# Second feed-forward product also as seven block products, two pairs of tiles at a time, with sums of the middle channels parked in DRAM

## The chip, the cores and the metric

One core of one Trainium2 chip runs the whole kernel. Times are device microseconds. A run's time is that of one execution; the kernel before is given by the median of three runs. One further execution was recorded by the hardware profiler, and all rows below come from it. PE is TensorE, DVE VectorE, ACT ScalarE, POOL GpSimd, SP SyncE; the DMAs are issued from SP's queue, those that add into their target from POOL's.

## The reference, cut to what matters

One layer of a hybrid decoder on 512 tokens with 1024 channels, float32. The mixers ahead are untouched by the change; it concerns the feed-forward part:

```
x = x + merged
gate, up = split(rms_norm(x, norm2_g) @ w_ffn_in, 2)    # (512,1024) @ (1024, 2*2816)
x = x + (silu(gate) * up) @ w_ffn_out                   # (512,2816) @ (2816,1024)
```

The weights come as float32 from DRAM. Every product is formed from three float32r products (high half of the weights by high half of the activations, high by low, low by high), so each 128x128 weight tile is split on the chip: ACT casts it to its high half, DVE subtracts that from the tile to get the low half, and PE multiplies.

## The kernel before, in words

All activations lie channels by tokens, so a matmul has a 128x128 weight tile as its stationary side and up to 512 tokens as its moving side. Up to the residual the kernel runs the mixers and w_out with `Dense.__call__` (L1292): 4 weight tiles are loaded with one DMA of 256 KB, split, and multiplied with all 512 tokens.

**The first product** uses `SevenProducts` (L1310): the two halves of the input channels, the two column blocks of a pair (one tile of gate columns, one of up columns) and the two halves of the tokens make a 2x2 by 2x2 block product, which needs seven block products and not eight. A block product here is a *piece*: 4 weight tiles, three matmuls each, of 256 tokens: 12 matmuls. The pieces come in the order p1, p5, p6, p3, p7, p2, p4 (`seven`, L1395). Their weights are: p1 block g0; p5 the sum s of two blocks, formed by a plain load and a DMA that adds the second block; p6 is s plus g0 (added in place by DVE, L1415); p3 is that plus g1; p7 is g0 plus another block, which a DMA adds into g0's buffer once p6 has read it (`third`, L1455); p2 is g1 and p4 is u1. The seven results are added up in the readers r1 to r4, and r4 multiplies silu(gate) by up and splits the result into the activations of the second product, kept in 11 arenas.

Two pairs run interleaved, piece by piece, 11 such couples for 22 pairs. The raw blocks lie in a ring of 12 buffers of 512 columns (L1359), the split ones in rings of 6; `run` (L1491) makes (adds, casts, subtracts) five pieces ahead of PE.

**The second product** (L1301 to L1303 with act) is plain: 8 output tiles by 22 input tiles by three matmuls of 512 tokens, 48 weight blocks with one DMA, one cast and one subtraction each. `take_out` (L1746) scales, adds the residual, which lies in DRAM, and writes.

Every engine runs its own list of instructions in order; a wait in front of one holds all behind it. The lists are made by a scheduler at build time, so they differ from the order in which the code issues.

Of the kernel before, what the change touches and what calls it, by code (L numbers as in the profile page):

```python
# [23 lines left out]
P = 128  # L24
# [67 lines left out]
class Env:  # L92


    def __init__(self, ctx, tc):
# [26 lines left out]
        self.pools["s"] = Slots("slot", self.early + cut(arenas[NARENA - 3:]))  # L122
# [61 lines left out]
    def leave_mixers(self):  # L184

        assert not self.scopes
        self.mctx.close()
        self.spool = self.later.enter_context(self.tc.tile_pool(name="fpool", bufs=1, reuse_waits="tile"))
        self.phase = "f"
        free = [b for n in ("pd", "prw", "ps") for b in self.pools[n].free]  # L190
        assert len(free) == 8
        for n, k in (("pd", 4), ("ps", 4)):
            self.pools[n] = Slots(n, [free.pop(0) for _ in range(k)])

# [1014 lines left out]
class Dense:  # L1209
# [23 lines left out]
    def ring(self, tag, dt, n):  # L1233

        tiles, at = self.rings.setdefault(tag, ([], [0]))
        if len(tiles) < n:
            at[0] = len(tiles)
            tiles.append((self.E.spool if self.E.phase else self.E.cpool).tile([P, KB * P], dt, name=self.E.uid(tag)))
        t = tiles[at[0] % len(tiles)]
        at[0] += 1  # L1240
        return t

# [67 lines left out]
class SevenProducts:  # L1310
# [10 lines left out]
    H, N, AHEAD = 4, 256, 5  # L1321

    def __init__(self, E, dense, act_hi, act_lo):
# [5 lines left out]
        self.raws, self.turn = None, 0  # L1329
# [26 lines left out]
    def block(self, w, k):  # L1356
        return self.dense.blocks(w, KD, P)[k]

    def raw(self):  # L1359

        E = self.E
        if self.raws is None:
# [7 lines left out]
    def load(self, w, k, t=None, add=False):  # L1370
        E, nc = self.E, self.E.nc
        t = self.raw() if t is None else t
        v = t.rearrange("p (k n) -> p k n", n=P)
        if add:
            nc.gpsimd.dma_start(v, self.block(w, k), accum_op=ALU.add)
        else:
            nc.sync.dma_start(v, self.block(w, k))
        return t

    def split(self, w):  # L1380
        d = self.dense
        hi, lo = d.ring("wh", F32R, WB[1] + 1), d.ring("wl", F32R, WB[1] + 1)
        self.E.split(w, hi, lo)
        return hi, lo

    def matmuls(self, ps, w, b, js, first, last):
        nc = self.E.nc
        for j in js:
            c = slice(j * P, (j + 1) * P)
            for n, (x, y) in enumerate(((0, 0), (0, 1), (1, 0))):  # L1390
                nc.tensor.matmul(ps, w[x][:, c], b(y, j), start=first and j == js[0] and n == 0,  # L1391
                                 stop=last and j == js[-1] and n == 2, skip_group_check=True)


    def seven(self, o, i, wg, wu):  # L1395
# [4 lines left out]
        act = lambda k, t: (lambda y, j: self.act[y][:, H * k + j, t])  # L1400
        tee = lambda i: (lambda y, j: self.t[y][:, i, j])

        def piece(name, make, bank, x, first, read):
            def mm():
                if bank not in o:
                    o[bank] = E._take("pf", (P, 512), True)
                self.matmuls(o[bank][:, 0:N], o[name], x, range(H), first, True)

            def mk():
                o[name] = self.split(make())  # L1410
            return mk, mm, read

        def sum_(other, after=None):
            def f():
                V.tensor_tensor(o["s"], o["s"], o[other], ALU.add)  # L1415
                if after:
                    after()
                return o["s"]
            return f

        def r1():
            o["k"], o["n"] = (E.slot("sp_k", keep=True) for _ in range(2))
            nc.scalar.copy(o["k"][:, a], o["x"][:, 0:N])  # L1423

        def r5():
            nc.scalar.copy(o["n"][:, b], o["y"][:, 0:N])

        def r6():
            nc.scalar.copy(o["k"][:, b], o["x"][:, 0:N])

        def r3():
            V.tensor_tensor(o["k"][:, b], o["k"][:, b], o["y"][:, 0:N], ALU.add)
            E.free(o["y"])

        def r7():
            nc.scalar.copy(o["n"][:, a], o["x"][:, 0:N])
            V.tensor_tensor(o["k"][:, b], o["k"][:, b], o["n"][:, b], ALU.add)
            V.tensor_tensor(o["n"][:, b], o["n"][:, a], o["n"][:, b], ALU.add)

        def r2():  # L1440
            V.tensor_tensor(o["k"][:, a], o["k"][:, a], o["v"][:, 0:N], ALU.add)
            E.free(o["v"])
            V.tensor_tensor(o["k"], o["k"], self.R, ALU.mult)
            nc.scalar.activation(o["k"], o["k"], AF.Silu)

        def r4():
            t, n = o["k"], o["n"]
            V.tensor_tensor(t[:, a], t[:, a], o["x"][:, 0:N], ALU.mult)
            E.free(o["x"])
            V.tensor_tensor(t[:, b], t[:, b], n[:, b], ALU.mult)  # L1450
            E.free(n)
            E.split(t, self.out[0][i], self.out[1][i], -1.0)
            E.free(t)

        def third():  # L1455
            self.load(wu, 0, o["g0"], add=True)

        return [piece("p1", lambda: o["g0"], "x", act(0, a), True, r1),
                piece("p5", lambda: o["s"], "y", act(0, b), True, r5),
                piece("p6", sum_("g0", third), "x", tee(0), False, r6),  # L1460
                piece("p3", sum_("g1"), "y", act(1, b), True, r3),
                piece("p7", lambda: o["g0"], "x", tee(1), False, r7),
                piece("p2", lambda: o["g1"], "v", act(1, a), True, r2),
                piece("p4", lambda: o["u1"], "x", tee(2), False, r4)]

    def first(self, f):
        for i in range(f, min(f + 2, len(self.pairs))):
            o, (wg, wu) = self.os[i], self.pairs[i]
            o["g0"], o["s"] = self.load(wg, 0), self.load(wu, 0)
            self.load(wu, 1, o["s"], add=True)  # L1470

    def rest(self, f):
        for i in range(f, f + 2):
            o, (wg, wu) = self.os[i], self.pairs[i]
            o["g1"], o["u1"] = self.load(wg, 1), self.load(wu, 1)

    def begin(self, pairs, n):


        self.pairs, self.os = pairs, [{} for _ in pairs]  # L1480
        self.pieces, self.at, self.made = [], {}, n
        for f in range(0, len(pairs), 2):
            self.at[len(self.pieces)] = f
            for both in zip(*[self.seven(self.os[i], i, *pairs[i]) for i in (f, f + 1)]):
                self.pieces += both
# [363 lines left out]
```

## Time and profile before

| | us |
|---|---|
| runs (median of 3; lowest to highest) | 1004.62 (1004.23 to 1010.87) |
| the profiled execution | 1011.66 |
| its span, first to last instruction | 1009.9 |
| its mean granted TensorE clock | 0.988 |

The profiled execution's own time is 1.74 us more than its span and 7.04 us above the median. Shares of busy time on the page are means over stages with different limits; the stages that matter here are the end of w_out (until 663.6 us in the span), the first product (to 885.7 us) and the second (to 1005.5 us).

### The profile page before, as it was taken

Reading aid. Unit: us, or ns where it says so; the run is one execution under the profiler, and the core shown is the slowest. Engines: PE = TensorE matmul, PEld = TensorE weight load, DVE = VectorE, ACT = ScalarE, POOL = GpSimd, SP = SyncE. Lnnn points to the kernel's source line nnn. Section 1 sums busy time; section 2 is a strip of 40 time slices with the busy share of each in tenths; the row PEclk is TensorE's granted clock in tenths of the full one; section 3 lists DMA queues with packets and bytes.
Section 4 is the critical chain, followed back from the end, with each engine's and each line's share of the span. In section 5 each row is a group of like instructions: output and inputs, shape, how many; then the busy total and the mean of one; then the engine's idle time right before and its main releaser. Section 6 shows DMA issues by size and latency. Waiting matters only on the chain.

```text
span 1009.9 us, 17883 instructions
## 1 busy us (share of the span) xinstructions
PE 970.1 (96%) x6416; PEld 824.2 (82%) x6416; DVE 754.3 (75%) x1941; ACT 473.5 (47%) x978; POOL 143.3 (14%) x176
## 2 busy tenths in 40 slices
PE   7989999899999999999999999989999999999998
PEld 5777777676779777888887788879999999988886
DVE  6899676789994789977867655679989998943331
ACT  6534333434342566446446324566666666632220
POOL 2021120422420001000000332011211221000000
PEclk9999899999998999999999999999999999999999
DMA  7325242221431334252448864476776677354440
GB/s 241 116 53 133 64 110 78 84 56 53 100 96 40 95 105 116 84 156 75 154 149 270 273 194 159 138 178 165 151 163 175 152 153 170 79 155 123 131 136 27
DMA packets 105593, 129.95 MB, mean 129 GB/s; under 512 B 45376, under 2 KB 47296, under 8 KB 105504
## 3 DMA queue, kind: packets, MB, share of 16 engines
q1 hardware_dynamic: 99168, 117.28, 38.7%
q0 software_dynamic: 6336, 11.54, 7.4%
q8 instruction: 50, 0.82, 0.3%
q14 instruction: 39, 0.32, 0.1%
HBM read 109.90 MB, written 18.88 MB: 128 GB/s over the span
## 4 chain that ended last, share of the span: by engine, by line
PE 77%; DVE 15%; DMA 3%; ACT 2%; issue 2%; POOL 1%; SPq 0%; DVEq 0%; ACTq 0%; POOLq 0%
PE bank L1391 21%; PE bank L1302 13%; PE bank L1303 13%; PE bank L1301 13%; DVE wl L1230 2%; DMA ar<-in_w_ffn_in 1%; DMA ar<-ymix 1%; PE bank L468 1%; PE bank L479 1%; PE bank L1188 1%; PE bank L262 1%; PE bank L630 1%; PE bank L1285 1%; PE bank L1286 1%; PE bank L1287 1%
## 5 line engine op out<-in xcount | busy, mean ns | idle before, releaser
L1229 ACT CAST wh<-wr 128x512 fp32r<-128x512 f32 x198 | 120.4, 611 | 208.8 <-PE bank L1302 163.6
L1230 DVE TENSOR_TENSOR wl<-wr,wh 128x512 fp32r<-128x512 f32 x198 | 136.8, 693 | 82.8 <-ACT wh L1229 82.3
L1301 PE MATMUL bank<-act_hi,wh 128*128 128x512 f32 x360 | 150.5, 418 | 7.8 <-ACT wh L1229 5.9
L1302 PE MATMUL bank<-act_lo,wh 128*128 128x512 f32 x360 | 149.7, 416 | 0.8 <-DVE act_lo L257 0.7
L1303 PE MATMUL bank<-act_hi,wl 128*128 128x512 f32 x360 | 149.6, 416 | 0.0
L1391 PE MATMUL bank<-sp_t,wh 128*128 128x256 f32 x528 | 97.5, 285 | 1.1 <-ACT ar L1423 0.8
L1391 PE MATMUL bank<-act_hi,wh 128*128 128x256 f32 x352 | 98.0, 278 | 0.0
L1391 PE MATMUL bank<-act_hi,wl 128*128 128x256 f32 x352 | 97.7, 278 | 0.1
L1391 PE MATMUL bank<-act_lo,wh 128*128 128x256 f32 x352 | 97.5, 277 | 0.0
L1301 PEld LDWEIGHTS bank<-act_hi,wh 128*128 128x128 f32 x360 | 70.0, 195 | 22.7 <-ACT wh L1229 5.9
L1391 PEld LDWEIGHTS bank<-sp_t,wh 128*128 128x128 f32 x528 | 82.7, 193 | 1.5 <-ACT ar L1423 1.0
L1302 PEld LDWEIGHTS bank<-act_lo,wh 128*128 128x128 f32 x360 | 70.0, 194 | 16.4 <-DVE act_lo L257 3.5
L1303 PEld LDWEIGHTS bank<-act_hi,wl 128*128 128x128 f32 x360 | 70.0, 194 | 14.4 <-issue 0.6
L1391 PE MATMUL bank<-sp_t,wl 128*128 128x256 f32 x264 | 75.2, 285 | 0.0
L1301 PE MATMUL bank<-act,wh 128*128 128x512 f32 x176 | 68.5, 389 | 0.0
L1302 PE MATMUL bank<-act,wh 128*128 128x512 f32 x176 | 68.5, 389 | 0.0
L1303 PE MATMUL bank<-act,wl 128*128 128x512 f32 x176 | 68.5, 389 | 0.0
L1391 PEld LDWEIGHTS bank<-act_hi,wl 128*128 128x128 f32 x352 | 66.2, 188 | 0.7 <-DVE wl L254 0.7
L1391 PEld LDWEIGHTS bank<-act_hi,wh 128*128 128x128 f32 x352 | 66.4, 189 | 0.3
L1391 PEld LDWEIGHTS bank<-act_lo,wh 128*128 128x128 f32 x352 | 66.4, 189 | 0.0
L253 ACT CAST wh<-ar 128x512 fp32r<-128x512 f32 x79 | 48.2, 622 | 28.1 <-DMA ar<-in_w_ffn_in 18.1
L254 DVE TENSOR_TENSOR wl<-ar,wh 128x512 fp32r<-128x512 f32 x79 | 53.1, 685 | 9.4 <-ACT wh L253 8.9
(491 smaller groups left out, 2217.7 us busy)
## 6 DMA issues: line engine op xcount, KB each, us to landing
wr<-in_w_in SPq DMA_DIRECT2D x88, 256.0 KB, 2.9
ar<-in_w_ffn_in SPq DMA_DIRECT2D x46, 256.0 KB, 3.2
wr<-in_w_ffn_out SPq DMA_DIRECT2D x40, 256.0 KB, 2.7
gate<-ar SPq DMA_DIRECT2D x24, 256.0 KB, 2.4
wr<-in_w_branch SPq DMA_DIRECT2D x24, 256.0 KB, 3.6
ar<-gate SPq DMA_DIRECT2D x24, 256.0 KB, 3.6
ar<-in_w_ffn_in POOLq DMA_DIRECT2D x22, 256.0 KB, 3.9
sp_raw<-in_w_ffn_in SPq DMA_DIRECT2D x21, 256.0 KB, 3.4
```

Of the source, the lines that this page charges most:

```text
L253: nc.scalar.copy(hi, src)
L254: nc.vector.tensor_tensor(lo, src, hi.bitcast(F32), ALU.subtract)
L262: self.nc.tensor.matmul(ps[:, b, :], sq[:, b * P:(b + 1) * P], self.c("sel"), start=True, stop=True)
L468: nc.tensor.matmul(pa[:, c * P:(c + 1) * P], kb[rows, 4 * q + c].rearrange("p a t -> p (a t)"), ar[rows, 4 * q + c].rearrange("p a t -> p ...
L479: nc.tensor.matmul(pt[64:128, w], aam[q][0:64, c, h, 1], uv[0:64, 4 * q + c, h * CH:(h + 1) * CH], start=True, stop=True)
L630: nc.tensor.matmul(pu[:, 0:P], yt[:, c0:c0 + 2].rearrange("p c t -> p (c t)"), ts, start=True, stop=True)
L1229: nc.scalar.copy(wh, raw)
L1230: nc.vector.tensor_tensor(wl, raw, wh.bitcast(F32), ALU.subtract)
L1301: nc.tensor.matmul(ps, wh[:, j], hi(k), start=k == 0, stop=False)
L1302: nc.tensor.matmul(ps, wh[:, j], lo(k), start=False, stop=False)
L1303: nc.tensor.matmul(ps, wl[:, j], hi(k), start=False, stop=k == nk - 1)
L1391: nc.tensor.matmul(ps, w[x][:, c], b(y, j), start=first and j == js[0] and n == 0, stop=last and j == js[-1] and n == 2, skip_group_check= ...
```

## The change

**First product.** A unit is now two pairs at once: 8 weight tiles (512 KB) per block, so 11 units of seven pieces with 24 matmuls of 256 tokens each. One cast, one subtraction and one addition work on 1024 columns. The raw ring has five buffers of 1024 columns, of which a unit takes four (g0, s, g1, u1); the split rings have three; the pieces are made two ahead of PE. At the end of a unit r4 also forms three sums over its middle channels (S, four subtractions and additions of 256 columns) and writes them to DRAM (`sp_sums`).

**Second product.** It is a block product too: two groups g of four output tiles, each as three units of 4, 4 and 3 input-tile pairs, seven pieces each; the pieces of a group add up in seven PSUM banks over its three units. p1, p2, p3 and p5 read the arenas, p6, p7 and p4 the parked sums, which `fetch` loads from DRAM (12 loads, each split by ACT and DVE) into act_hi, act_lo and sp_t. Readers come only in a group's last unit.

**Elsewhere.** The rings wr, wh, wl of all stages are now halves of double buffers.

```diff
@@ Dense
-            tiles.append((self.E.spool if self.E.phase else self.E.cpool).tile([P, KB * P], dt, name=self.E.uid(tag)))
+            whole = [self.E.cpool.tile([P, 2 * KB * P], dt, name=self.E.uid(tag)) for _ in range((n + 1) // 2)]
...
+    def pair(self, tag):
+        r = self.rings[tag]
+        t = r["whole"][r["pair"] % len(r["whole"])]
+        r["pair"] += 1
+        return t
@@ SevenProducts
-    H, N, AHEAD = 4, 256, 5
+    H, N, AHEAD = 4, 256, 2
...
-            self.raws = [E.slot("sp_raw", keep=True) for _ in range(6)]
-            self.raws += [E.spool.tile([P, KB * P], F32, name=f"sp_raw{i}") for i in range(3)]
-            self.raws += self.dense.rings["wr"][0]
+        self.raws = [E.spool.tile([P, 2 * KB * P], F32, name=f"sp_raw{i}") for i in range(3)] + dense.rings["wr"]["whole"]
...
+        def make(src, other=None, after=None):
+            def f():
+                if other:
+                    V.tensor_tensor(u[src][:, 0:n], u[src][:, 0:n], u[other][:, 0:n], ALU.add)
+                if after:
+                    after()
+                d = self.dense
+                hi, lo = d.pair("wh")[:, 0:n], d.pair("wl")[:, 0:n]
+                E.split(u[src][:, 0:n], hi, lo)
+                return hi, lo
...
+        return [piece("p1", make("g0"), "p1", new),
+                piece("p5", make("s"), "p5", new),
+                piece("p6", make("s", "g0", third), "p6" if own else "p1", new and own),
+                piece("p3", make("s", "g1"), "p3" if own else "p5", new and own),
+                piece("p7", make("g0"), "p7" if own else "p1", new and own),
+                piece("p2", make("g1"), "p2", new),
+                piece("p4", make("u1"), "p4" if own else "p1", new and own)]
+    def unit_in(self, j, blocks, arenas):
...
+        def r4():
+            V.tensor_tensor(ka, ka, bank("p1"), ALU.mult)
+            E.free(u["banks"].pop("p1"))
+            V.tensor_tensor(kb, kb, nb, ALU.mult)
+            V.tensor_tensor(K[:, 4], K[:, 1], K[:, 0], ALU.subtract)
+            V.tensor_tensor(S[:, 1], K[:, 3], K[:, 0], ALU.subtract)
+            V.tensor_tensor(S[:, 0], K[:, 3], K[:, 4], ALU.add)
+            V.tensor_tensor(S[:, 2], S[:, 0], K[:, 2], ALU.subtract)
+            E.split(K[:, 1:5].rearrange("p s n -> p (s n)"), arenas[j][:, 0:4 * N], arenas[j][:, 4 * N:8 * N], -1.0)
+            nc.sync.dma_start(self.sdr[:, :, j].rearrange("s p n -> p s n"), S)
...
+    def fetch(self, i, c):
+        k = min(4, KF // 2 - 4 * c)
+        t = (self.k[1], self.n[1])[self.fetched % 2][:, 0:k]
+        self.fetched += 1
+        nc.sync.dma_start(t, self.sdr[i, :, 4 * c:4 * c + k])
+        hi, lo = self.place(i, c)
+        E.split(t.rearrange("p s n -> p (s n)"), hi[:, 0:k * N], lo[:, 0:k * N], 1.0 if i == 0 else -1.0)
...
+    def fill(self, i, name):
+        if i < len(self.units) and name not in self.units[i]:
+            u = self.units[i]
+            u[name] = self.load(u["blocks"][dict(g0=0, s=1, g1=3, u1=2)[name]])
+            if name == "s":
+                self.load(u["blocks"][2], u["s"])
@@ run
+            for k in range(made, min(i + self.AHEAD + 1, len(pieces))):
+                if k % 7 == 0:
+                    self.fill(k // 7, "g1")
+                    self.fill(k // 7, "u1")
+                    self.fill(k // 7 + 1, "g0")
                 pieces[k][0]()
+                if k % 7 == 4:
+                    self.fill(k // 7 + 1, "s")
+                made += 1
@@ trunk_kernel
-    for d in range(KD):
-        dense(A["w_ffn_out"][d], KF, lambda k: ah[k], lambda k: al[k], take_out(d))
```

**DVE's list, at the seam of two units of the first product.** The kernel before, two interleaved pairs a and b: L1448 is r4's product with the bank of p4, L1415 the addition for p6 or p3, L254 the subtraction that gives a piece's low half, L257 that of the arena.

```order
L254 TENSOR_TENSOR wl_149<-ar_12_80,wh_148 128x512
L1448 TENSOR_TENSOR ar_14_82<-ar_14_82,bank_88 128x256
L1415 TENSOR_TENSOR ar_14_82<-ar_14_82,ar_13_81 128x512
L1448 TENSOR_TENSOR ar_13_81<-ar_13_81,bank_84 128x256
L257 SCALAR_TENSOR_TENSOR act_6046<-ar_14_82,act_6046 128x512
L254 TENSOR_TENSOR wl_5991<-ar_14_82,wh_5990 128x512
```

And now, between units 2 and 3, from behind the low half of p5 of unit 3 (whose s is wr_102, whose g0 is sp_raw_5669): L1489 and L1487 are r4's products, L1491, L1490, L1492 and L1493 its sums, L263 the arena's low half, L1415 the additions for p6 and then p3, and L260 the low halves of p6, p7 and p3 of unit 3.

```order
L1489 TENSOR_TENSOR ar_12_80<-ar_12_80,ar_14_82 128x2x256
L1487 TENSOR_TENSOR ar_12_80<-ar_12_80,bank_83 128x512
L1491 TENSOR_TENSOR ar_12_80<-ar_12_80 128x256
L1490 TENSOR_TENSOR ar_12_80<-ar_12_80 128x256
L1415 TENSOR_TENSOR wr_102<-wr_102,sp_raw_5669 128x1024
L1492 TENSOR_TENSOR ar_12_80<-ar_12_80 128x256
L263 SCALAR_TENSOR_TENSOR act_6025<-ar_12_80,act_6025 128x1024
L1493 TENSOR_TENSOR ar_12_80<-ar_12_80 128x256
L260 TENSOR_TENSOR wl_109<-wr_102,wh_106 128x1024
L1415 TENSOR_TENSOR wr_102<-wr_102,wr_103 128x1024
L260 TENSOR_TENSOR wl_108<-sp_raw_5669,wh_105 128x1024
L260 TENSOR_TENSOR wl_107<-wr_102,wh_104 128x1024
```

Where one product with the bank of p4 stood ahead of the addition for p6 of 512 columns, two products of 512 and two sums of 256 now stand ahead of one of 1024; and the low half of p7 (wl_108) stands ahead of that of p3 (wl_107), though PE multiplies p3 first.

**POOL's list, the DMAs that add, in the same stretch.** Before, each row another buffer of the ring:

```order
L1375 DMA ar_14_82<-in_w_ffn_in 128x512
L1375 DMA ar_12_80<-in_w_ffn_in 128x512
L1375 DMA ar_13_81<-in_w_ffn_in 128x512
L1375 DMA wr_135<-in_w_ffn_in 128x512
L1375 DMA wr_102<-in_w_ffn_in 128x512
```

And now, from unit 0 on: two in a row go into the same buffer, first the third block into g0 of a unit (for its p7), then the second block of s of the next unit (for its p5), which reuses that buffer.

```order
L1399 DMA sp_raw_5667<-in_w_ffn_in 128x1024 x2
L1399 DMA wr_103<-in_w_ffn_in 128x1024 x2
L1399 DMA wr_102<-in_w_ffn_in 128x1024 x2
L1399 DMA sp_raw_5669<-in_w_ffn_in 128x1024 x2
L1399 DMA sp_raw_5668<-in_w_ffn_in 128x1024 x2
```

Before, s of a couple of pairs lay in buffers that had been free for longer; now s of the next unit can be loaded only when p7 of this one has been split.

## Rows read from the trace of the kernel before

**Rows 1.** The page's head and its section 1: busy time, share, instructions.

```profile
span 1009.9 us, 17883 instructions
PE 970.1 (96%) x6416; PEld 824.2 (82%) x6416; DVE 754.3 (75%) x1941; ACT 473.5 (47%) x978; POOL 143.3 (14%) x176
```

**Rows 2.** Chain of work that ended last: start, us, what; its end.

```profile
661.18 4.40 DMA ar<-in_w_ffn_in
...
685.83 190.01 PE bank L1391 x1631
875.88 9.88 PE bank L1391 x82
1005.51 0.70 DVE ar L1751
1006.23 0.69 DVE ar L1752
```

**Rows 3.** Windows: us, PE, PEld, DVE, ACT, POOL busy (instructions), PEclk, DMA, GB/s.

```profile
700.00:720.00 20.00, 20.00 (x174) 20.00 (x174) 18.40 (x36) 13.24 (x27) 3.48 (x4) 1.00 0.72 172
885.50:1005.50 120.00, 119.97 (x531) 99.02 (x529) 38.86 (x63) 26.69 (x47) 0.00 (x0) 1.00 0.39 115
```

**Rows 4.** Timeline of PE at w_out's end: start, us, idle time before it.

```profile
658.52 0.50 PE L1303 MATMUL bank<-mg,wl 128*128 128x512 f32 x1 [1.99 <-DVE wl L1230]
...
663.64 0.28 PE L1391 MATMUL bank<-act_hi,wl 128*128 128x256 f32 x1
```

**Rows 5.** Timeline of DVE in the first product, at a seam.

```profile
787.27 0.41 DVE L1448 TENSOR_TENSOR ar<-ar,bank 128x256 f32<-128x256 f32 x1
787.60 0.68 DVE L1415 TENSOR_TENSOR ar<-ar,ar 128x512 f32<-128x512 f32 x1
788.20 0.41 DVE L1448 TENSOR_TENSOR ar<-ar,bank 128x256 f32<-128x256 f32 x1
```

**Rows 6.** Groups by line and form: the 1024-column operations, us and mean ns.

```profile
L285 DVE TENSOR_TENSOR rw_wl<-ar,rw_wl 32x1024 fp32r<-32x1024 f32 x1 | 1.2, 1222 | 0.0
L283 ACT CAST rw_wl<-ar 128x1024 fp32r<-128x1024 f32 x1 | 1.1, 1053 | 0.0
```

**Rows 7.** DMA, 680 to 880 us: queues (packets, MB, share); issues (KB, us to landing).

```profile
q0 software_dynamic: 5472, 9.96, 32.5%
q1 hardware_dynamic: 11016, 20.05, 31.8%
...
sp_raw<-in_w_ffn_in SPq DMA_DIRECT2D x18, 256.0 KB, 3.3
ar<-in_w_ffn_in POOLq DMA_DIRECT2D x18, 256.0 KB, 3.9
sp_raw<-in_w_ffn_in POOLq DMA_DIRECT2D x10, 256.0 KB, 4.2
```

**Rows 8.** DMA issues of the first 40 us: KB each, us to landing.

```profile
const<-in_consts SPq DMA_DIRECT2D x1, 513.0 KB, 4.7
...
ar<-in_w_lora SPq DMA_DIRECT2D x1, 512.0 KB, 5.8
...
ar<-in_s_b SPq DMA_DIRECT2D x1, 256.0 KB, 4.6
```

**Rows 9.** Line L1375, the DMAs that add, all 44 of them.

```profile
DMA to landing us min/median/max: 3.6/4.0/6.7
```

**Rows 10.** Timeline of ACT in the first product: a cast that waits.

```profile
795.19 1.14 ACT L253 CAST wh<-ar 128x512 fp32r<-128x512 f32 x2 [1.43 <-DMA ar<-in_w_ffn_in]
```

**Rows 11.** Windows around two idle stretches of PE, columns as in Rows 3.

```profile
183.00:187.00 4.00, 0.70 (x4) 0.52 (x4) 3.86 (x6) 0.14 (x1) 2.16 (x3) 1.00 0.00 0
187.00:191.00 4.00, 4.00 (x15) 3.35 (x14) 3.31 (x8) 1.95 (x5) 1.12 (x2) 0.58 0.49 113
656.00:659.00 3.00, 1.01 (x6) 0.72 (x5) 1.82 (x4) 1.14 (x2) 0.00 (x0) 1.00 0.72 220
659.00:662.00 3.00, 3.00 (x15) 2.47 (x14) 2.63 (x6) 2.02 (x4) 0.82 (x2) 1.00 0.99 337
```

More of the change, by code (lines that the diff above doesn't have):

```diff
@@ L1368, in raw, with load @@
         return t
[L1370 to L1375, printed above, removed]
+    def load(self, w, t=None):
+        nc = self.E.nc
+        if t is None:
+            t = self.raw()
+            nc.sync.dma_start(t[:, 0:w.shape[1]], w)
         else:
-            nc.sync.dma_start(v, self.block(w, k))
+            nc.gpsimd.dma_start(t[:, 0:w.shape[1]], w, accum_op=ALU.add)
@@ L1378, in load @@
         return t
[L1380 to L1392, printed above, removed]
@@ L1413, in sum_ @@
[L1413 to L1419, printed above, removed]
+        K, Nn, S = self.k[j % 2], self.n[j % 2], self.sums
+        ka, kb, na, nb = K[:, 1:3], K[:, 0:4:3], Nn[:, 0:2], Nn[:, 2:4]
+        u = dict(blocks=blocks, h=H, banks={}, own=False, new=True, last=True)
+        bank = lambda name: u["banks"][name].rearrange("p (t n) -> p t n", n=N)
@@ L1466, in first @@
[L1466 to L1485, printed above, removed]
-        self.first(0)
-        self.rest(0)
-        for i in range(n):
-            self.pieces[i][0]()
@@ L1491, in run @@
-    def run(self, norm, ah, al):
-        self.out, n = (ah, al), self.made
-        self.first(2)
-        pieces = self.pieces
-        for i in range(len(pieces)):
-            for k in range(self.made, min(i + (n if i < n else self.AHEAD) + 1, len(pieces))):
-                if k in self.at:
-                    self.rest(self.at[k])
-                    self.first(self.at[k] + 2)
+            V.tensor_tensor(na, kb, bank("p7"), ALU.add)
+            E.free(banks.pop("p7"))
+            V.tensor_tensor(kb, kb, nb, ALU.add)
@@ new lines, in begin, with run @@
+    def begin(self, units):
+        self.units, self.fetched = units, 0
+        self.pieces = [p for u in units for p in self.seven(u)]
+        for name in ("g0", "s", "g1"):
+            self.fill(0, name)
+        for k in range(self.AHEAD):
+            self.pieces[k][0]()
+        self.dense.last_singles()
+    def run(self, norm, between):
+        pieces, made = self.pieces, self.AHEAD
+        self.fill(0, "u1")
+        self.fill(1, "g0")
+        for i in range(len(pieces)):
+            for k in range(made, min(i + self.AHEAD + 1, len(pieces))):
[3 more added lines that the diff above has]
+                    self.fill(k // 7 + 1, "g0")
@@ L1522, in add @@
         with E.scope("s"):
[L1523 removed]
+            sq = self.into if self.into is not None and self.n == 0 else E.slot("rsq", keep=True)
             E.nc.scalar.activation(sq, x, AF.Square)
```

251 lines of the change are left out of this document (164 added, 87 removed).

## The prediction

> **What bounds the kernel now.** I read the page's shares first: PE is busy for 96% of the span and DVE for 75% [rows 1]. Then the chain of waits: it ends in TensorE alone, 190.01 us in one stretch in the first product and 9.88 at its end, and then two DVE operations and a write [rows 2]. Then the windows, because shares mix stages. In 20 us of the first product PE is busy for all 20 with 174 matmuls, 0.115 us each, and the clock is full; DVE is busy for 18.40 of these 20 and waits only a little. In the second product 531 matmuls of 512 tokens fill 120.00 us, and DVE has 38.86 to do [rows 3]. So TensorE sets the time; splitting is nearly as much work in the first product, but runs ahead of it. What should be seen beside this: the casts already wait for DMAs that add, 1.43 us in the row shown [rows 10]. With five pieces of lead nobody notices.
>
> Times below are summed against the profiled execution, 1011.66 us (span 1009.9 and 1.74 around it). It lies 7.04 above the median of the runs, 1004.62.
>
> **The parts of the change.**
>
> *Rings as halves of double buffers.* The stages up to w_out issue what they did, with as many buffers. 0.
>
> *Start of the first product.* The first matmul of 256 tokens starts at 663.64 [rows 4] and the last ends at 885.76 (875.88 + 9.88, [rows 2]): 222.1 us. Eleven couples of 14 pieces of 12 are 1848 matmuls, at 0.115 us 212.4. So 9.7 us are lost, nearly all before 685.83, where the chain's unbroken stretch begins [rows 2]. And w_out loses 1.99 at its end, waiting for a low half [rows 4], while DMA is busy to 0.99 [rows 11]. Now the first blocks are in buffers of their own and can be split before w_out ends. Of these 11.7 I leave 1.7 for a first unit that starts cold: **-10** (bounds: -4, if its blocks come no sooner, and -11.7).
>
> *First product, matmuls.* 11 units of 168, as many as before: 19.3 us a unit, nothing changes.
>
> *First product, DVE.* A 256-wide operation follows the last after 0.33 us, a 512-wide after 0.60 [rows 5], 0.08 less than they last; the 1024-wide one lasts 1.22 [rows 6], so 1.14. A unit has ten of 1024, seven of 512, four of 256: 11.4 + 4.2 + 1.3 = 17 us of 19.3. The work fits; the four sums cost nothing by themselves. What matters is order: the lead is two pieces, and both DVE and the raw buffers are taken in a fixed order. Two loops go through a unit.
>
> *Price of the DMAs.* No block of 512 KB is loaded or added under load before. For 256 KB the plain load lands after 3.3 us, the adding one after 3.6 at least and 4.0 in the middle [rows 7, 9]. Queue q1 was busy for 31.8% of 200 us with 20.05 MB, or 76.5 such blocks: 0.83 us of all engines each; q0 32.5% with 38: 1.71 us each [rows 7]. Doubled, a plain load is 3.3 + 0.83 = 4.1. For the adding one I take the least landing, since now each on POOL's queue waits for the one ahead to be used and has no other ahead of it: 3.6 + 1.71 = 5.3. Bounds: below, the 513 KB that landed in 4.7 beside 256 KB in 4.6 [rows 8] say that size costs little, 3.5 and 4.3; above, 4.7 for the plain load and the longest adding one, 6.7 [rows 9]. I stay near the engine times, because they are measured in the stage itself.
>
> The Trainium skill has a rule for this (DMA: Bandwidth & Descriptors, "Anatomy of one DMA — SWDGE (gpsimd) path"): about 2.0 us fixed and the bytes at 436,000 per us. By it 256 KB more cost an estimated 0.6 us, not 1.71; the adding DMA would be 4.6 to 4.7, the load 3.9. The trace's 1.71 speaks against it for adding DMAs, without a run of 512 KB that decides.
>
> *Loop A, the buffer of g0.* s of the next unit goes where g0 of this unit lay, so it can load only when p7 is split. From the end of p5's low half: r4's two products and two sums 0.60 + 0.60 + 0.33 + 0.33, the addition for p6 1.22: 3.1. Then the third block is added into g0: 5.3. Cast (1.05, [rows 6]) and low half of p7: 2.3. Plain load of s: 4.1. Adding its second block: 5.3. Cast and low half of p5: 2.3. That is **22.4 us** where TensorE needs 19.3.
>
> *Loop B, DVE's order.* p7's low half stands ahead of p3's, though PE wants p3 first. From PE's end of p4: one product, two sums and the addition for p6, 0.60 + 0.67 + 1.22 = 2.5; third block 5.3; cast 1.05; low half of p7 1.14, of p3 1.22; then PE does p3, p7, p2 and p4, 4 x 2.76 = 11.0, of which 0.23 (the two matmuls on the high half) could go ahead. Sum 16.7 + 5.3 = **22.0 us**. So everything behind the cast of p7 on ACT, and the low half of p3 on DVE, waits for a DMA that p3 doesn't need.
>
> The longer loop sets the period: 22.4 - 19.3 = 3.1 us at each of ten hand-overs, **+31**. Both loops lie so close that mending one would give back only 0.4.
>
> The parking writes (384 KB a unit) and the loads of s leave DMA at some 0.7 to 0.8 busy as now [rows 3]; that cover is gone only if they meet the adding DMAs, which the upper bound holds.
>
> *Second product.* 2 groups x 11 pairs of input tiles x 7 pieces x 6 matmuls (two tiles, three each) are 924 of 256 tokens: 106.2 us at 0.115, where 120.0 are spent now [rows 3]: -13.8. Its loop A lacks r4's 1.9: 20.5. Hand-overs: from the last unit in, 3.1; to the second unit 20.5 - 19.3 = 1.2; to the third, whose blocks are a quarter smaller, 0; to the next group 4.7, since TensorE needs only 14.5 for a third unit against 19.2; then 1.2 and 0: 10.2. Here p3 is split ahead of p7, so there is no loop B. Together **-3.6**. The weights are 17.3 MB against 11.5 before, and 12 loads bring back 5.8 MB of sums, so a DMA share of 0.39 [rows 3] becomes some 0.75; what waits for these loads I leave to the range (0 to +10).
>
> *Tail.* Two operations of DVE of 512 columns and a write, as now [rows 2]: 0.
>
> Sum: -10 + 31 - 3.6 = **+17.4**, 1029 us in an execution like the profiled one, **1022 on the median**.
>
> **The rivals.**
> 1. *Size costs a DMA little* (3.5 and 4.3). Loop A 19.8, B 21.0: B sets the period, +17. The second product keeps 0.5 and 2.1 of its excess: -11.2. With -10: -4, **1000**. For it: the 513 KB [rows 8]; against it: the queue's engine time. By the skill's rule (4.7 and 3.9) it would be B 21.4, +21, -8.8 in the second product, about 1007, much the same case. Chance 0.22.
> 2. *Faster: the adding DMA is never the late one.* Loop B fits in 19.3 if the third block lands within 2.6 us of the addition for p6, or if the low half of p3 is not held behind it as I read the order; A fits if both adding DMAs and the load land in 11.6 together (19.3 less 7.7 of ACT and DVE). Then only the gains stay: -10 and -13.8, **981**. At the least landing seen, 3.6 with 3.3 for the load, B is 20.3: +10, **991**. Against it: no adding DMA of half the size landed in under 3.6 [rows 9]. Chance 0.16.
> 3. *The clock.* After an idle stretch in which PE worked 0.70 of 4 us, the next 4 us had a granted 0.58, between the two levels 1.2 and 2.4 GHz, 1.7 us lost; after one in which it worked 1.01 of 3 the clock stayed full [rows 11]. If each stall of about 3 us is followed by the first, +17 more: **1039**. A stall here is as long as these two; that the engine is fully busy before and after speaks against. Chance 0.11.
> 4. *Transfers at their dearest* (4.7, 6.7): loop A 25.8, +65; the second product +16.8; **1076**. Chance 0.09.
>
> **How the numbers follow.** My forecast has 0.42. About 1% (10 us) is what a measurement of this kernel can tell from no change. Below 994.6 lies rival 2 and an edge of rival 1: 0.20. Between 994.6 and 1014.7 most of rival 1 and the forecast's lower edge: 0.24. Above: 0.56. The range leaves out rival 2's best (981) and rival 4, and reaches from 988 to 1055. The forecast's own range is 1010 to 1040.
>
> **What the new profile would show.** In the first product PE idle once a unit for about 3 us, ahead of p3's matmuls, released by DVE's low half; ACT's cast of p7 waiting for the adding DMA; adding DMAs of 512 KB landing after about 5.3 us, loads after 4.1; a period of 22.4 us and 243 us from first to last matmul. An idle stretch ahead of p5 instead means that loop A, not B, is what TensorE meets. The second product would take some 116 us, with the longest stall where the second group starts. A start within 2 us of w_out's end confirms the -10. The prediction fails if 512 KB land in under 4.5 us, if PE's stalls sit elsewhere (loads of parked sums in the second product, a full ring of split blocks), or if PE's clock drops behind each stall.

## The result, and the profile after

| | us |
|---|---|
| kernel before, median of 4 runs | 1007.5 (1004.23 to 1010.87) |
| changed kernel, median of 4 runs | 1081.78 (1075.99 to 1084.0) |
| ratio, with its 95% interval | 1.0728 (1.0665 to 1.0792) |

The change makes the kernel 74 us slower. Forecast were 1022 and a range of 988 to 1055. The profiled execution is the quickest of the four, 1075.99. Its head and section 1, to be read against [rows 1]:

```profile
span 1074.2 us, 18161 instructions
PE 981.6 (91%) x6812; PEld 848.3 (79%) x6812; DVE 804.5 (75%) x1832; ACT 482.9 (45%) x845; POOL 134.6 (13%) x166
```

PE fell from 96% to 91%; no other engine rose in its place. So TensorE waits. Where, is read from its timeline. First the ends of the stages: before, the first matmul of w_out and that of the second product, and then of the changed kernel the first of w_out, the first and two later ones in the first product, the first of the second product, and its last (columns: start, us, what, idle before it and its releaser):

```profile
617.60 0.39 PE L1301 MATMUL bank<-mg,wh 128*128 128x512 f32 x1
...
885.60 0.40 PE L1301 MATMUL bank<-act,wh 128*128 128x512 f32 x1
```

```profile
607.99 0.39 PE L1322 MATMUL bank<-mg,wh 128*128 128x512 f32 x1
...
651.51 0.28 PE L1442 MATMUL bank<-act_hi,wh 128*128 128x256 f32 x1
...
665.77 0.29 PE L1442 MATMUL bank<-act_hi,wh 128*128 128x256 f32 x1
...
914.20 0.39 PE L1442 MATMUL bank<-act_hi,wh 128*128 128x256 f32 x1 [2.06 <-ACT wh L259]
...
926.59 0.40 PE L1442 MATMUL bank<-act,wh 128*128 128x256 f32 x2
...
1065.47 0.28 PE L1442 MATMUL bank<-act_hi,wl 128*128 128x256 f32 x1
```

665.77 is p3 of unit 0 and 914.20 p3 of unit 10: ten hand-overs in 248.4 us, 24.84 each, where TensorE needs 19.3 by the prediction's price of a matmul. w_out and the first product together took 268.0 (617.60 to 885.60) and take 318.6; the second product 119.5 (885.60 to the last matmul, 1005.08) and now 138.9; the tail to the span's end 4.8 and now 8.7. The stages ahead of w_out, which issue the same instructions, ended 9.6 us earlier in this execution; the other kernels below, with the same stages, end them between 608.0 and 617.6, so that is no effect of the change. -9.6 + 50.6 + 19.4 + 3.9 is the 64.3 by which the spans differ, and without the -9.6 it is the 74 of the medians.

The stalls of three units, and one period of the chain of waits (columns: start, us, what), unit to unit, with ACT's row from it:

```profile
736.86 0.39 PE L1442 MATMUL bank<-act_hi,wh 128*128 128x256 f32 x1 [2.32 <-ACT wh L259]
...
761.99 0.39 PE L1442 MATMUL bank<-act_hi,wh 128*128 128x256 f32 x1 [2.27 <-ACT wh L259]
...
787.41 0.55 PE L1442 MATMUL bank<-act_hi,wh 128*128 128x256 f32 x1 [2.24 <-ACT wh L259]
```

```profile
754.37 5.56 DMA sp_raw<-in_w_ffn_in
759.95 1.05 ACT wh L259
761.02 1.24 DVE wl L260
762.28 3.75 DMA sp_raw<-in_w_ffn_in
...
766.56 7.31 DMA sp_raw<-in_w_ffn_in
773.97 1.06 ACT wh L259
775.06 0.99 DVE wl L260
...
778.15 1.14 DVE sp_raw L1415
...
779.82 5.52 DMA sp_raw<-in_w_ffn_in
```

```profile
759.95 1.99 ACT L259 CAST wh<-sp_raw 128x1024 fp32r<-128x1024 f32 x2 [4.00 <-DMA sp_raw<-in_w_ffn_in]
```

The last row is ACT's: the cast of p7, where [rows 10] had a wait of 1.43 that nobody noticed, now waits 4.00 for the third block, and with it that of p3 (x2). The rows before are loop A, step by step as it was foretold: third block, p7's split, load of s, its adding DMA, p5's split, the addition for p6, and the next third block, 25.45 us after the last. No TensorE is in it.

The chain runs round A like this in four of the ten hand-overs (729.19 to 805.61 and 857.24 to 882.39). In the other six it leaves A at the cast of p3 and goes over TensorE: its matmuls up to the end of p7, the cast that waits for these, and DVE's list up to the low half of the next p5. One of these, from third block to third block, 24.39 us:

```profile
882.39 5.32 DMA sp_raw<-in_w_ffn_in
...
890.72 7.05 PE bank L1442 x47
...
897.79 1.06 ACT wh L259
...
901.95 1.22 DVE wl L260
...
906.78 5.35 DMA sp_raw<-in_w_ffn_in
```

A is hardly shorter there: the addition into s had landed at 900.64, and in the period above 1.2 us lie between that landing and p5's low half (773.87 to 775.06), so the low half at 901.95 came only 0.1 us later than A alone would have had it. Worked out in the same way it is 0.1 to 1.3 us in five of the six and 2.3 in the first, 5.2 together. So both ways set the time, and A is never far from it.

What the two adding DMAs had beside them shows on the queues (SP's, then POOL's, same stretch):

```profile
755.67 0.38 SPq L1495 DMA_DIRECT2D sp_sums<-ar  x1
762.28 1.46 SPq L1397 DMA_DIRECT2D sp_raw<-in_w_ffn_in  x2
764.55 6.29 SPq L1397 DMA_DIRECT2D wr<-in_w_ffn_in  x2
```

```profile
754.37 0.86 POOL L1399 DMA_DIRECT2D sp_raw<-in_w_ffn_in  x1 [12.29 <-DVE ar L1492]
766.56 0.86 POOL L1399 DMA_DIRECT2D sp_raw<-in_w_ffn_in  x1 [11.33 <-DMA sp_raw<-in_w_ffn_in]
```

The third block at 754.37 has only a parking write beside it: 5.56. The addition into s at 766.56 follows loads of g1 and u1 of 512 KB each, issued in the 4 us ahead of it, and one of the next g0 comes some 4 us behind: 7.31. Over the units the third block takes 5.3 to 6.0 us (6.5 in unit 0) and the addition into s 5.9 to 7.6. DMA from 680 to 880 us answers to [rows 7] (queues; then issues, KB, median us to landing):

```profile
q1 hardware_dynamic: 7808, 19.93, 29.7%
q0 software_dynamic: 2304, 8.39, 25.4%
...
sp_raw<-in_w_ffn_in SPq DMA_DIRECT2D x19, 512.0 KB, 4.5
wr<-in_w_ffn_in SPq DMA_DIRECT2D x13, 512.0 KB, 4.9
wr<-in_w_ffn_in POOLq DMA_DIRECT2D x8, 512.0 KB, 5.9
sp_raw<-in_w_ffn_in POOLq DMA_DIRECT2D x8, 512.0 KB, 6.4
```

As many bytes a second as before at most, and the queues are no busier; the transfers come in bursts with nothing between (a DMA share of 0.00 from 902 to 904 us). In the second product the loads of parked sums are in the burst too, and the chain's adding DMAs are longer still:

```profile
918.57 9.73 DMA sp_raw<-in_w_ffn_out
...
947.11 8.93 DMA wr<-in_w_ffn_out
```

Last, the tail, answering to [rows 2]: DVE's last operation.

```profile
1070.35 0.69 DVE L1587 TENSOR_TENSOR ar<-ar 128x512 f32<-128x512 f32 x1
```

The last matmul started at 1065.47; DVE had just begun one operation and had eight more of some 0.6 us to do, where there were two.

### The profile page after: what moved, and what is told of

It is laid out like the page before. It is cut to its first block, busy times and chain, and to the rows that moved or that the text cites. A ratio compares the mean times of both kernels' runs of the same rounds, so it can differ in the third digit from the quotient of the medians.

```text
span 1074.2 us, 18161 instructions
## 1 busy us (share of the span) xinstructions
PE 981.6 (91%) x6812; PEld 848.3 (79%) x6812; DVE 804.5 (75%) x1832; ACT 482.9 (45%) x845; POOL 134.6 (13%) x166
## 4 chain that ended last, share of the span: by engine, by line
PE 46%; DVE 23%; DMA 19%; ACT 6%; issue 4%; POOL 1%; SPq 0%; ACTq 0%; DVEq 0%; POOLq 0%
PE bank L1323 9%; PE bank L1324 8%; PE bank L1322 8%; DMA sp_raw<-in_w_ffn_in 8%; PE bank L1442 5%; DVE wl L260 4%; DMA sp_raw<-in_w_ffn_out 4%; ACT wh L259 4%; DMA wr<-in_w_ffn_out 3%; DMA wr<-in_w_ffn_in 2%; DVE wl L1236 2%; DVE sp_raw L1415 1%; PE bank L474 1%; DMA ar<-ymix 1%; PE bank L1194 1%
## 5 line engine op out<-in xcount | busy, mean ns | idle before, releaser
L1442 PE MATMUL bank<-act_hi,wh 128*128 128x256 f32 x440 | 131.2, 298 | 26.1 <-ACT wh L259 25.0
L1235 ACT CAST wh<-wr 128x512 fp32r<-128x512 f32 x150 | 92.3, 620 | 125.1 <-PE bank L1323 90.1
L259 ACT CAST wh<-sp_raw 128x1024 fp32r<-128x1024 f32 (+1 forms) x74 | 74.9, 1025 | 130.3 <-PE bank L1442 42.6
L260 DVE TENSOR_TENSOR wl<-sp_raw,wh 128x1024 fp32r<-128x1024 f32 (+1 forms) x74 | 87.4, 1193 | 59.1 <-ACT wh L259 58.0
L1442 PE MATMUL bank<-act_hi,wl 128*128 128x256 f32 x440 | 129.1, 293 | 1.0 <-DVE wl L260 1.0
L1442 PE MATMUL bank<-act_lo,wh 128*128 128x256 f32 x440 | 128.4, 292 | 0.0
L1236 DVE TENSOR_TENSOR wl<-wr,wh 128x512 fp32r<-128x512 f32 x150 | 107.3, 718 | 12.3 <-ACT wh L1235 11.7
L260 DVE TENSOR_TENSOR wl<-wr,wh 128x1024 fp32r<-128x1024 f32 (+1 forms) x45 | 53.0, 1186 | 38.5 <-ACT wh L259 38.4
L1324 PEld LDWEIGHTS bank<-act_hi,wl 128*128 128x128 f32 x360 | 68.2, 189 | 13.8 <-issue 0.6
L259 ACT CAST wh<-wr 128x1024 fp32r<-128x1024 f32 (+1 forms) x45 | 45.5, 1020 | 69.2 <-PE bank L1442 32.3
L1442 PE MATMUL bank<-act,wh 128*128 128x256 f32 x352 | 67.9, 292 | 5.3 <-ACT wh L259 5.3
```

The source lines that it names most:

```text
L259: nc.scalar.copy(hi, src)
L260: nc.vector.tensor_tensor(lo, src, hi.bitcast(F32), ALU.subtract)
L1235: nc.scalar.copy(wh, raw)
L1236: nc.vector.tensor_tensor(wl, raw, wh.bitcast(F32), ALU.subtract)
L1324: nc.tensor.matmul(ps, wl[:, j], hi(k), start=False, stop=k == nk - 1)
L1442: E.nc.tensor.matmul(ps[:, t * self.N:(t + 1) * self.N], w[a][:, c], x(b, j), start=first and t == 0 and j == 0 and i == 0, stop=u["last"] ...
```

## The experiments

Stages from the timelines of PE: "first" is w_out and the first product, from w_out's first matmul to the second product's first; "second" from there to the last matmul. Ratios are to the kernel before on the same chip.

| run | us | ratio (interval) | first | second |
|---|---|---|---|---|
| before | 1007.5 | | 268.0 | 119.5 |
| changed | 1081.78 | 1.0728 (1.0665 to 1.0792) | 318.6 | 138.9 |
| e1_order | 1089.43 | 1.0788 (1.0742 to 1.0833) | 323.4 | 144.2 |
| e2_sins | 1095.04 | 1.0824 (1.0778 to 1.0869) | 335.1 | 138.6 |
| e3_both | 1070.79 | 1.0587 (1.055 to 1.0625) | 312.1 | 135.1 |
| e4_noadd | 1014.15 | 1.0043 (1.0015 to 1.0071) | 272.9 | 117.0 |
| e5_s2 | 1038.39 | 1.0275 (1.0196 to 1.0353) | 280.3 | 132.0 |
| e6_pool | 1036.62 | 1.0291 (1.0245 to 1.0337) | 283.7 | 128.6 |
| e7_nofetch | 1072.39 | 1.0658 (1.0616 to 1.0699) | 318.7 | 130.9 |
| e8_s2 | 1032.58 | 1.0241 (1.0197 to 1.0285) | 279.1 | 128.8 |
| e9_six | 1023.88 | 1.0161 (1.0102 to 1.022) | 271.8 | 126.7 |
| e10_late | 1023.86 | 1.0165 (1.012 to 1.021) | 265.8 | 133.5 |
| e11_defer | 1021.64 | 1.0156 (1.0111 to 1.02) | 265.8 | 129.3 |
| e12_plain2 | 1005.33 | 0.9976 (0.995 to 1.0002) | 267.9 | 119.5 |
| e13_first_only | 1050.37 | 1.0439 (1.0382 to 1.0496) | 310.8 | 119.5 |

The theory was the two loops. The rivals (numbered 1 and 2 in the expectations below, apart from those of the prediction) were: the traffic as a whole; the order of ACT and DVE alone.

**e1_order**: p7's split is issued behind p3's.

```diff
-                E.split(u[src][:, 0:n], hi, lo)
+                with ExitStack() as st:
+                    for x in u.get("behind", ()) if behind else ():
+                        st.enter_context(E.tc.issue_after(x))
+                    x = E.nc.scalar.copy(hi, u[src][:, 0:n])
+                    y = V.tensor_tensor(lo, u[src][:, 0:n], hi.bitcast(F32), ALU.subtract)
+                if other == "g1":
+                    u["behind"] = (x.ins, y.ins)
```

> Only change to the new kernel: on ACT and DVE the split of p7 is issued behind that of p3. Theory (two loops, A through g0's buffer with two adding DMAs and a load, B through the order): A alone is enough for the period of 25.4 us, so little is gained: 0 to 10 us under the new kernel, some 1070 to 1082; the stall of 2.3 us ahead of p3 moves to p5 or p6. Rival 1 (the total traffic of the DMAs is the limit): no change. Rival 2 (order of ACT and DVE alone, with a lead of two pieces): the 2.7 us a unit ahead of p3 are won back, 1050.

The 0 to 10 us were not gained; the time is some 8 us above the changed kernel's, with overlapping intervals. The chain now runs round A without TensorE in each hand-over looked at, 26.0 to 26.4 us (740 to 845 us). The order alone (rival 2) is not it.

**e2_sins**: s goes into s's own buffer, and is loaded behind p3's split.

```diff
-        t = self.raws[self.turn % len(self.raws)]
+        if name == "s":
+            return self.raws[0]
+        t = self.raws[1 + self.turn % (len(self.raws) - 1)]
...
-                if k % 7 == 4:
+                if k % 7 == 3:
```

> Only change: s of the next unit is loaded into the buffer of this unit's s (free when p3 is split) and not into g0's (free when p7 is split); the order stays, with p7's low half ahead of p3's. Theory: s still waits behind the third block, through the order, and one low half more (1.2 us a unit): 0 to +12 us, 1076 to 1092, less what s's adding DMA wins where fewer loads run beside it (up to 1.8 a unit). Rival 1 (traffic): no change. Rival that loop A alone counts, B not: a period of 22.7, 1055.

13 us more, just beyond the expected range's end (by the ratios some 10, with intervals that touch). In the chain from 740 to 845 us s waits for one more low half (1.2), and its load takes 4.4 to 5.8 us where it took 3.4 to 3.8; additions into s of 5.9 to 7.6 don't make up for that. A loop A without B's order would have given 1055; it didn't.

**e3_both**: the two edits together.

> Both edits together: p3 split ahead of p7, and s loaded into s's own buffer. Theory: now no loop holds both adding DMAs; s's goes from the end of p5 over one copy, one cast, one low half, load 4.3, add 5.5 to 7.3 and another split to p5 of the next unit, 18.1 to 19.9 us; the third block has 10.8 of 11.0 us. Period 19.5 to 20.5 where it was 25.4, so 50 to 60 us less in the first product and 5 to 15 in the second: 1005 to 1027. Rival 1 (traffic is the limit): less than 15 us won, over 1060. Rival 2 (DVE and ACT in order are the limit whatever the DMAs do): a period of 22 or more, 1040.

A miss: 11 us won, not 55 to 77. The third block was out of the chain, but what replaced it was no shorter. Three periods of its chain, and SP's queue beside them:

```profile
741.43 9.79 DMA sp_raw<-in_w_ffn_in
...
768.73 9.88 DMA sp_raw<-in_w_ffn_in
...
794.52 8.88 DMA sp_raw<-in_w_ffn_in
```

```profile
763.20 3.97 SPq L1399 DMA_DIRECT2D sp_raw<-in_w_ffn_in  x3
769.33 0.33 SPq L1399 DMA_DIRECT2D wr<-in_w_ffn_in  x1
```

The addition into s took 7.3 us in the period shown of the changed kernel and 8.9 to 9.9 in these three (7.1 to 9.9 over the units), with the loads of g1 and u1 issued ahead of it (the last two of the three at 763.20; the first is s's own) and that of the next g0 0.6 us behind (0.3 to 2.3). Beside it stands order: from the end of p5's low half to the load of s are 9.8 us of DVE's and ACT's lists (780.77 to 790.59). By this run rival 1 (traffic) could still be right.

**e4_noadd**: no adding DMAs.

```diff
-            if name == "s":
-                self.load(u["blocks"][2], u["s"])
...
-            self.load(u["blocks"][1], u["g0"])
+            pass
```

> The new kernel without any adding DMA (neither the second block of s nor the third block in g0), in both products; all else as it is, so that its weights are not those of the block products. Theory: what remains of a loop is load and splits, the order of DVE and ACT alone gives at most 20.3 us a unit: 50 to 60 less in the first product, 15 to 25 in the second, 1000 to 1015. Rival 2 (order and lead, not DMAs): more than 1040. Rival 1 (traffic): somewhere between, since a third of the bytes are gone.

1014, 68 us less: 45.7 in the first part, a little under the 50 to 60, and 21.9 in the second product. The adding DMAs, with what waits for them, are what the time goes to. A period is 20.67 us, and p3 still waits 0.47 for a low half.

**e6_pool**: as e3, but g1, u1 and the next g0 come from POOL's queue, behind the addition into s.

```diff
-            nc.sync.dma_start(t[:, 0:w.shape[1]], w)
+            q = nc.sync if name == "s" or not self.at else nc.gpsimd
+            with self.E.tc.issue_after(self.last.ins) if q is nc.gpsimd else ExitStack():
+                q.dma_start(t[:, 0:w.shape[1]], w)
```

> As e3_both, but g1, u1 and the next g0 are loaded from POOL's queue, behind the DMA that adds into s, where SP issued them beside it. Theory (the loads beside it make it 9.4 us, alone it takes 5.2): s's adding DMA back to 5.2 to 6 us, e3's loop 25.8 - 4 = 21.5 to 22.3 us: 35 to 45 us less than e3's 1071, 1026 to 1036. If an adding DMA of 512 KB is just that slow, or all traffic is the limit: as e3, over 1060.

1036.6, 34 us under e3 with the same bytes, at the expected range's end. In the chain the additions into s:

```profile
739.83 5.57 DMA sp_raw<-in_w_ffn_in
...
763.13 5.40 DMA sp_raw<-in_w_ffn_in
```

Over the units they take 5.1 to 5.6 us, 6.3 once. So e3's 9.8 were the loads beside, neither size nor total traffic: rival 1 falls. The edit changed both the loads' queue and their place in time; no run tells which of the two does it.

**e5_s2** and **e8_s2**: as e3, the raw buffers given out so that s has two, and the loads issued one a piece, behind p3, p7, p2 and p4. (The lines are e8's; in e5 the first unit multiplied other weights.)

```diff
+        self.turn[name] = i = self.turn.get(name, 0) + 1
+        return self.raws[{'g0': (1, 1), 's': (3, 0), 'g1': (2, 2), 'u1': (4, 4)}[name][i % 2]]
...
+                for m, name, d in ((3, "s", 1), (4, "g0", 1), (5, "g1", 1), (6, "u1", 1)):
+                    if k % 7 == m:
+                        self.fill(k // 7 + d, name)
```

> As e3_both (p3 split ahead of p7), but the five raw buffers are given out otherwise: two alternate for s, one each for g0, g1 and u1. s can then be loaded a unit ahead, and g0 of the next unit waits for p7's split. Theory (an adding DMA costs 5.2 us alone and up to 9.9 beside three loads, and e3's loop of 25.8 us held one of 9.4): s's adding DMA is in no loop; the third block's loop is 2.5 + 0.5 + 5.3 + 2.3 + 4.3 + 2.3 = 17.2 us. Period about 20.7 as without adding DMAs, to 22 where loads lie beside the third block: 1015 to 1035. If traffic as such is the limit: above 1060, like e3.

> As e5_s2 with the five raw buffers given out so that the first unit's g1 lies outside the ring that w_out still uses (in e5_s2 the last loads of w_out fell into it, so unit 0 worked on other weights). No other difference: as e5_s2, 1026 to 1040; the first product at 21.3 to 21.9 us a unit, bound by the third block's way through g0's buffer into the next unit's first piece.

1038, a little above 1015 to 1035, and 1033, inside 1026 to 1040. The chain now goes from the third block over p7's split to the next g0 and p1, 21.2 to 21.8 us in e8: the one-buffer g0 is the last loop that holds an adding DMA.

**e9_six**: a sixth raw buffer for g0, which is now loaded two units ahead.

```diff
-        return self.raws[{'g0': (1, 1), 's': (3, 0), 'g1': (2, 2), 'u1': (4, 4)}[name][i % 2]]
+        return self.raws[{'g0': (5, 1), 's': (4, 0), 'g1': (2, 2), 'u1': (3, 3)}[name][i % 2]]
```

> As e8_s2 with a sixth raw buffer, so that g0 alternates between two as s does (room for it by halving the DMA scratch). Theory: now no adding DMA and no buffer lies in a loop of less than two units; the order of DVE and ACT is what is left, 20.7 us a unit as without adding DMAs: 6 to 12 us under e8_s2, 1015 to 1028, and the stall ahead of p3's low half of 0.5 us stays as in e4_noadd. If e8_s2's period was set by something else (traffic, DVE's order): no change.

1023.9, 9 us less, as expected. p3's stalls, two units apart:

```profile
750.67 0.39 PE L1447 MATMUL bank<-act_hi,wl 128*128 128x256 f32 x1 [0.47 <-DVE wl L1423]
...
791.98 0.39 PE L1447 MATMUL bank<-act_hi,wl 128*128 128x256 f32 x1 [0.47 <-DVE wl L1423]
```

41.31 us for two: 20.66 a unit, what e4 had without any adding DMA. They are no shorter, as line L1399's equal shows from 690 to 870 us, but all hidden:

```profile
DMA to landing us min/median/max: 5.3/6.3/9.6
```

**e7_nofetch**: the loads of the parked sums left out.

```diff
-        nc.sync.dma_start(t, self.sdr[i, :, 4 * c:4 * c + k])
...
+        return
```

> The new kernel without the 12 loads of the parked sums and their splits in the second product (p6, p7 and p4 multiply what lies there). Theory: they cost by lengthening the adding DMAs beside them (8.9 and 9.7 us at the second product's start, 5.2 alone) and by two splits that wait: 5 to 12 us, 1070 to 1077. If the second product's loss of 19 us against the kernel before is mostly this parking: 15 to 20 us, 1062 to 1067. If it is only its own loop A: 0 to 3.

7.9 us less in the second product and nothing in the first; 9 in the median, as expected. The two adding DMAs of 9.73 and 8.93 us take 6.71 and 5.75 here.

**e10_late** and **e11_defer**: r4's sums behind p3 of the next unit; then also the first group's last readers behind the second group's first splits.

```diff
+                if k % 7 == 3 and k > 7 and "sums" in self.units[k // 7 - 1]:
...
+                        self.units[k // 7 - 1]["sums"]()
```

> As e9_six, and r4's four sums, the split into the arena and the parking write are issued behind p3 of the next unit (they stood ahead of its low halves on DVE). Theory: the 20.67 us a unit of e9_six and e4_noadd are TensorE's 19.3 and the wait of p3 for DVE: from the end of p4 one product, two sums, the addition for p6, S0, the arena's low half, S2, p6's low half, the next addition and its split, some 9.5 us against 8.3. Without 3.3 us of these it fits: 19.3 to 19.6 us, 10 to 13 us under e9_six's 1024: 1010 to 1016. If the 20.67 are something else (weights that load late, the clock): as e9_six.

> As e10_late, and the first group's last readers in the second product (11 operations of DVE of 512 columns, 6.6 us) are put behind p6 and p3 of the second group's first unit; the load of its parked sums for p4 moves behind them. Theory: the stall of 3.1 us at the groups' seam goes, that of 4.0 before p7 (its adding DMA takes 8 us beside loads) stays: 2 to 4 us under e10_late, 1007 to 1013, level with the kernel before. If the seam only moves to p3: 0.

The first part falls by 6.0 to 265.8, under the kernel before (19.5 to 20.1 us a unit from the third on, where 19.3 to 19.6 were expected), but the second product rises by 6.8, so the medians stay: what DVE puts off at the end of the first product meets the second's first splits (stalls of 2.39, 1.20 and 3.71 us there). In this, e10's 10 to 13 us were missed. e11 wins some of it back (129.3); its median, 1021.6, misses the 1007 to 1013.

**e12_plain2** and **e13_first_only**: the second product plain again, with the first mended (e12), or as it was in the change (e13).

```diff
-            nc.sync.dma_start(self.sdr[:, :, j].rearrange("s p n -> p s n"), S)
...
-        units += [sp.unit_out(g, c, blocks_out(g, c), arenas, banks, x2dr, outT) for c in range(3)]
+        dense(A["w_ffn_out"][d], KF, act(0), act(1), take_out(d))
```

> The first product as in e10_late (six raw buffers, p3 ahead of p7, the split into the arena behind p3 of the next unit), the second product plain as in the kernel before (no sums, no parking). Theory: mended, the first product with w_out takes 265 to 266 us where the kernel before takes 268; the second 120, the tail as before: 0 to 4 us under the kernel before, 1002 to 1007. If the second product as blocks were worth something once the first is mended, this would be slower than e11_defer's 1022.

> The new kernel with only its second product undone: plain, as in the kernel before; so no sums and no parking either, the first product's loads, orders and buffers untouched. Theory: the traces put 19 us on the second product and 4 on the tail; the first product keeps its loops, less r4's sums and the parking writes beside the third block (1.3 us of DVE a unit in loop A): 1082 - 23 - 5 to 13 = 1046 to 1055. If the first product's loss comes from the parking (its writes beside the adding DMAs): 1030 or less.

e13 is 31 us under the changed kernel, as expected; the first product's loops stay without parking (first part 310.8). e12 is level with the kernel before, as expected (ratio 0.9976, the interval just takes in 1). Windows of the changed kernel's first product, then of e12's (columns as in [rows 3]):

```profile
700.00:780.00 80.00, 70.14 (x551) 67.61 (x550) 57.37 (x71) 36.27 (x42) 5.35 (x7) 0.96 0.52 134
780.00:860.00 80.00, 69.64 (x522) 67.04 (x521) 55.09 (x67) 35.23 (x42) 5.87 (x7) 0.91 0.54 135
```

```profile
700.00:780.00 80.00, 78.73 (x671) 77.92 (x670) 65.36 (x77) 45.13 (x60) 6.91 (x8) 1.00 0.63 159
780.00:860.00 80.00, 78.73 (x671) 77.92 (x670) 65.37 (x77) 45.13 (x60) 6.06 (x7) 1.00 0.60 152
```

The same kind of pieces, PE busy for 78.7 of 80 us in place of 70, with more bytes a second (152 to 159 GB/s in place of 134).

## Why the prediction was wrong

Of the 56.5 us between the forecast's +17.4 and the stages' 73.9, 29.6 lie in w_out and the first product (50.6 for 21), 23.0 in the second product, 3.9 in the tail. By its own steps:

- *What bounds it, and loop A*: right in the main. The stall is ahead of p3, 2.0 to 2.7 us in nine of ten units, released not by DVE's low half but by ACT's cast of p3, which stands behind that of p7. Loop A's steps are the chain's in four hand-overs, and it has nearly the chain's length in the others. That mending loop B alone gives almost nothing back, as it said, is what e1 showed.
- ***Price of the DMAs***: **the step that failed.** It took the least landing for the adding DMA, since on POOL's queue each would have no other ahead of it: 5.3. That holds for the third block (5.3 to 6.0) and, with the loads moved behind it, for s (5.1 to 5.6, 6.3 once, in e6). It forgot SP's queue: s's addition is issued just behind the loads of g1 and u1 and takes 5.9 to 7.6 behind those two, 7.1 to 9.9 where the next g0's load comes close behind as well (e3). It said that "cover is gone only if they meet the adding DMAs" and left that to the upper bound. In the period shown: 22.4 + 2.0 (s) + 0.2 (third) - 0.35 (load) + 1.06 (twice 0.53 from a release to the issue on POOL, which no term had) + 0.1 = 25.4.
- *Rival 4, transfers at their dearest* (4.7 and 6.7): it gave loop A 25.8 and 1076, got 0.09 and lay outside the range. Its size is right, its terms are not: the load (3.75) and the third block (5.56) were cheaper, the addition into s (7.31) dearer, and the 1.06 were missing. That these cancel is luck.
- *+31 for ten hand-overs*: 24.84 us measured for 19.3, +55. The 19.3 is itself a little low: 0.115 us a matmul comes from a window's count, which takes in those that reach over its edges. The chain's 190.01 us for 1631 matmuls [rows 2] are 0.1165, or 19.6 a unit.
- *-10 at the start*: -6. The first blocks did come in time: the first matmul of the first product stands at 651.51, without a stall behind w_out. But from w_out's first matmul to p3 of unit 0 are 57.8 us (607.99 to 665.77), of which 192 matmuls of 0.226 and three pieces of 2.76 are 51.6: 6.2 lost, where the kernel before lost 12.1 over both stages. What the prediction allowed for the cold first unit, 1.7, was too little. At 0.1165 a matmul less was lost before, and only some 3 us were won.
- *Second product, -3.6*: +19.4. Here the step that failed is "what waits for these loads I leave to the range": e7 gives 7.9 us to the loads, e4 21.9 to the adding DMAs, and these overlap, since the loads lie beside them (9.73 and 8.93). The longest stall stands not where the second group starts (3.25 us) but in the first unit: 5.43 us ahead of 941.31. There p7 is cast ahead of p3 (940.21 and 943.68), against the prediction's order, and the first two matmuls of p7, which wait for the third block, stand in PE's list ahead of the rest of p6. What the rest of the second product's loss is made of stays open.
- *Tail, 0*: +3.9. DVE's last readers were not counted.
- *Four sums that cost nothing by themselves*: so it was beside loops of 25 us. With these gone, DVE's order is what is left: 20.66 us a unit in e9, 19.5 to 20.1 with the sums later (e10).
- *Rival 3, the clock*: what it describes did come. Behind the stall ahead of p3 the granted clock was 0.50 to 0.73 over the next 3.5 to 3.8 us in eight of ten units, 1.00 in two. One of them, from p3's first matmul, and the stretch after it (columns as in [rows 3]):

```profile
889.77:893.30 3.53, 3.31 (x13) 3.02 (x14) 2.53 (x3) 1.38 (x2) 0.00 (x0) 0.52 0.52 167
893.30:896.80 3.50, 3.50 (x31) 3.50 (x31) 1.66 (x3) 1.05 (x1) 0.86 (x1) 1.00 0.92 303
```

Nearly all of the first stretch is at 1.2 GHz, with matmuls 0.21 us apart, the second at 2.4 with 0.12. Loop A has no matmul in it, so in its four hand-overs this costs nothing; in the other six it lies in the chain, but A would take over after the 5.2 us named above, an estimate of the most that a full clock could win in the first product. In e1, whose chain runs round A, the clock falls as well (0.93 from 690 to 860 us); e9 and e12 have 1.00 with stalls of 0.5 us and less. How much of it counts in the second product is not settled.

*Rival 2* is excluded: the quickest adding DMA of 512 KB in the first product of any run took 5.07 us (e3). *Rival 1*, that size costs little, was right for the load of s (3.4 to 3.8 where it had 3.5 and the forecast 4.1) and wrong for the adding DMAs (4.3).

The Trainium skill's rule that was weighed (DMA: Bandwidth & Descriptors, "Anatomy of one DMA — SWDGE (gpsimd) path") adds an estimated 0.6 us for 256 KB more; it is stated for DMAs from POOL's queue, so the prediction's 3.9 for a load from SP's goes beyond it. The least landing was 3.6 for 256 KB [rows 9]; for 512 KB, from 700 to 890 us of the changed kernel:

```profile
DMA to landing us min/median/max: 5.3/5.9/7.6
```

1.7 us more, as the queue's engine time had it and not the rule. By neither would the forecast have been 1082: the neighbours made the rest.

## What to carry to other kernels

A transfer's price is that of its place: ask what the same release lets loose on the other queues, and take the landing beside those, not the least one. When a lead is cut, follow each buffer once around until it is its own predecessor; a loop without the bounding engine in it can set the time however idle everything looks. Here two things cut it: the loads issued behind the addition (e6, 34 us), and each adding DMA taken out of a loop that short by another buffer (e8 and e9, 38 and 47 us under e3). Saved matmuls (13.8 us by the prediction's count) are worth only what the added splits, sums and loads leave: even behind a mended first product the second as blocks took 127 to 133 us against 119.5.

## What was not expected

An adding DMA of 512 KB takes some 5.4 us or up to 9.9 with the same three plain loads around it: 7.1 to 9.9 where they are on SP's queue, two ahead and one close behind (e3), 5.1 to 5.6, once 6.3, where the first of them follows 0.5 us behind on its own queue (e6). From the landing of s's load to the issue of the addition on POOL 0.53 us pass in the changed kernel (766.03 to 766.56), 0.29 in its first three units; for the third block it is 0.53 from the end of the addition for p6 (779.29 to 779.82).
